# A hybrid DeltaNet and attention step: one triangular inversion split by columns between two engines, masks and an inverse root on VectorE, value products with two heads in turn

## The chip, the core and the metric

The kernel is one program on one core of a Trainium2 chip. The metric is the device time of one execution in microseconds; lower is better. The core's engines each run their own queue of instructions in order and wait for one another through semaphores: TensorE (PE, matmuls and transposes; its weight loads are PEld in the profile), VectorE (DVE), ScalarE (ACT), GpSimd (POOL) and SyncE (SP), on whose queue most of the DMA transfers are issued. Some DMAs are issued from POOL's queue.

## The reference, cut to what matters

Two layers run over 640 tokens, 128 prompt tokens and 512 sample tokens (a grid of 8 rows of 64), of width 1024. Layer 0 mixes tokens by a bidirectional gated DeltaNet (8 heads), layer 1 by neighbourhood attention (16 heads). A gated ConvFFN follows each. All is float32.

```python
# layer 0, per head and direction, chunks of tokens
diff = gc[..., :, None] - gc[..., None, :]            # cumulated log decay
decay = where(lower, exp(where(lower, diff, 0)), 0)
a_mat = where(strict, einsum(kb, kc) * decay, 0)
t_mat = triangular_solve(eye + a_mat, eye, lower=True)
u, w = t_mat @ (vc * bc), t_mat @ (kb * exp(gc))
# then a scan over the chunks with state S: v_new = u - w @ S; o = ...; S = ...
o = rmsnorm(o_f + rev(o_b), norm_g) * silu(z)
# layer 1, per head: latent queries read a window of the grid and all 128 context keys
p = softmax(concat([s_loc + bias (masked), s_ctx]))
out = p_loc @ v_window + p_ctx @ v_ctx
```

## The kernel before

**Staging.** PE does the projections, the FFN and all products. A dense float32 product is three passes (L385 to L387): the weights and the activations are each split into a high part, rounded to the PE's fp32r type, and the rest; ACT makes the high part of a weight tile, DVE the rest by a subtraction (L375, `wl<-wst,wh`).

**Layer 0** has tokens in NBLK = 5 blocks of 128. Its work is a list of steps, written by hand. A letter is a kind of step, a digit the head (for I, the pair of heads):

```python
SCHED = (
    "k1 k0 K0 K1 k2 q0 K2 k3 a1 v1 K3 I0 a1 Q0 v0 V0 I1 q1 M0 v2 Q1 S0 V1 M1 V2 M2 S1 a3 z0 z1 q2 k4 F0 "
    "Q2 k5 F1 K4 K5 v3 z2 V3 a2 q3 Q3 S2 q4 v4 M3 I2 Q4 a2 V4 k6 z3 F2 M4 S3 K6 k7 K7 F3 S4 a1 q5 z4 M5 "
    "q7 a1 v5 Q5 v7 V5 I3 a2 v6 q6 F4 Q6 z5 a1 M6 V6 S5 Q7 z6 S6 M7 V7 F5 S7 a1 F7 F6 a1 z7"
)
```

- k, q, v, z are a head's projections with their convolution (tiles `dkT`, `dqT` and so on); a is a tile of the modulation map.
- **K** is `decay` and `keys`. `decay` (L678) builds a 128x1280 tile `dec` of decay differences in both directions: transposes on PE, additions on DVE (L698), a triangular mask on POOL (L702, two `affine_select` of 128x640, which write -1e30 outside the triangle), and the exponential on ACT (L708). `keys` (L764) turns the keys to tokens (`k3tp`, `k3ts` for head 3; `to_tokens` at L735 to L742), multiplies keys by keys (`kk3p`, `kk3s`, `pair` at L755 to L761), and DVE evicts the product with `dec` into M (L786). MT is its transpose (L791). M's and MT's 32x32 diagonal blocks are stored to a DRAM scratch `md` (L795, SP).
- **I** is `invert` (L799), for two heads at a time: 2 heads x 2 directions x 20 blocks = 80 partitions, each with one unit triangular 32x32 matrix. SP loads `lN` from `md` (L806). Then POOL runs 31 steps of two instructions, a product with broadcast operands into `lP` (L813) and an addition into the inverse `lY` (L819). POOL stores `lY` to `yd` (L820), transposes it by a copy (L821) and stores that to `wd` (L822).
- **M** is `merge` (L824): SP loads the inverted blocks from `yd` and `wd` into M and into small tiles `W6` and `Wx` (L834 to L841; the profile names `W6` as `W`), POOL clears parts of `W6` (L829, L830), and PE combines the 32x32 blocks to 128x128 (L848; tiles `p1` to `p5`, `p` in the profile).
- **Q** multiplies queries by keys into `dec` (L890), **V** scales the values (L900), **S** is the scan over the blocks (L908, tiles `sp`, `sb`), which also stores the final states (L940, SP).
- **F** is `finish` (L976): sums of squares of the output (ACT), then on DVE four small steps and a reciprocal on 128x5 tiles `so`, the power -1/2 on POOL (L989), and the scaling of the output `osb` by it on DVE (L991); PE transposes the result (`ot`, `otp`).

Each engine's order is set by a scheduler, which places an instruction by its priority: steps of kind S, M, K and I are raised by `PR`, and what is raised goes ahead of what is ready with it. Within an engine the order is fixed once built.

**Layer 1** takes the heads in 8 pairs and for each pair four column groups (`attend`, L1243). For a group, PE makes scores against window keys and context keys, for both heads in turn (L1263 to L1273; `skn`, `kc`); DVE and ACT do the softmax (L1184, `sts`); PE transposes the weights (L1312 for the window, `t`; L1315 for the context, `tc`), which are evicted to `ptw` (DVE) and `ptc` (ACT); PE multiplies them by the values into `no` (L1321 to L1330): first all three products of head 0 (two of the window with `vw`, one of the context with `cv`), then the three of head 1. The heads use different halves of the PE array's columns (`tile_position`). The scores of the next group are issued ahead of this group's transposes.

Of the kernel before, what the change touches and what calls it, by code (L numbers as in the profile page):

```python
# [13 lines left out]
F32R = mybir.dt.float32r  # L14
AF = mybir.ActivationFunctionType
# [19 lines left out]
PR = {"S": 2000, "I": 100, "M": 500, "K": 200}  # L35
# [544 lines left out]
class Gdn:  # L580
# [17 lines left out]
    def tokens(self):  # L598
# [4 lines left out]
        for t, sgn in ((self.UT, 1), (self.LT, -1)):  # L603
# [3 lines left out]
            )  # L607
        abT = self.gp.tile([128, W], F32, tag="kT", name="abT", bufs=4)
# [69 lines left out]
    def decay(self, h):  # L678
# [23 lines left out]
        for d, sgn in ((0, 1), (1, -1)):  # L702
            nc.gpsimd.affine_select(
                out=t[:, d], in_=t[:, d], pattern=[[0, NBLK], [sgn, 128]], compare_op=ALU.is_ge, fill=-1e30,
                base=0, channel_multiplier=-sgn,
            )
# [92 lines left out]
    def invert(self, nh, md, yd, wd, name):  # L799
# [5 lines left out]
        P = self.gp.tile([128, 256], F32, tag="lP", name=f"lP{name}", bufs=1)  # L805
# [4 lines left out]
        for i in range(31, 0, -1):  # L810
            n = 32 - i
            pr = P[:L, : i * n].rearrange("p (j c) -> p j c", c=n)
            nc.gpsimd.tensor_tensor(  # L813
                pr,
                N[:L, :i, i : i + 1].to_broadcast([L, i, n]),
                Y[:L, i : i + 1, i:].to_broadcast([L, i, n]),
                ALU.mult,
            )
            nc.gpsimd.tensor_tensor(Y[:L, :i, i:], Y[:L, :i, i:], pr, ALU.add)  # L819
# [156 lines left out]
    def finish(self, h):  # L976
# [4 lines left out]
        so = gp.tile([128, 4, NBLK], F32, tag="so", name=f"so{h}", bufs=2)  # L981
        for b in range(NBLK):
            nc.scalar.activation(sq[:, b], osb[:, b], AF.Square, accum_out=so[:, 0, b : b + 1])
        nc.vector.tensor_scalar(so[:, 1], ssq, 128.0, None, ALU.mult)
        nc.vector.reciprocal(so[:, 2], so[:, 1])
        nc.vector.tensor_tensor(so[:, 0], so[:, 0], so[:, 2], ALU.mult)
        nc.vector.tensor_scalar(so[:, 0], so[:, 0], 1.0 / 128, EPS, ALU.mult, ALU.add)
        nc.vector.tensor_tensor(so[:, 0], so[:, 0], so[:, 1], ALU.mult)
        nc.gpsimd.tensor_tensor(so[:, 3], so[:, 0], self.net.mhalf[:, :NBLK], ALU.pow)  # L989
# [33 lines left out]
    def run(self):  # L1023
# [4 lines left out]
        def step(op, h):  # L1028
# [14 lines left out]
            elif op == "I":  # L1043
                self.invert(2, *scr[h], h)
# [17 lines left out]
        for t in SCHED.split():  # L1062
            if t[0] in PR:
                with net.tc.high_priority(PR[t[0]]):
                    step(t[0], int(t[1]))
# [85 lines left out]
class Na:  # L1151
# [91 lines left out]
    def attend(self, p):  # L1243
# [51 lines left out]
        for cb in range(4):  # L1295
# [25 lines left out]
            for e in range(2):  # L1321
# [322 lines left out]
```

## Time and profile before

| what | value |
|---|---|
| median of 3 runs | 1900.02 us (1899.34 to 1905.55) |
| the profiled execution | 1899.56 us, span 1897.9 us |
| mean granted TensorE clock | 0.977 |
| weight loads on PE (PEld) | 1710.2 us (90%) |
| whole DeltaNet layer's inversions on POOL | 114.5 to 157.0, 188.1 to 227.6, 318.8 to 357.9, 431.9 to 471.9 us |
| DMA, mean | 102 GB/s |

The span is cut by the page into 40 slices of 47 us. Layer 0's mixer fills about the first 12 of them, layer 1's attention lies from 1110 to 1385 us, and most of the rest is FFN, where PE's three passes (L385 to L387) are the costliest groups. In rows of a timeline the columns are the start, the duration, the engine, the line, the operation, the output from the inputs with their sizes, how often, and in brackets the idle time of the engine before it with what ended it. In the list of waits the numbers behind the colon are the sum of the idle time, how often, and the longest.

### The profile page before, as it was taken

The numbers are of one execution on the slowest core, as the hardware profiler recorded it, in microseconds if no ns is written. First come the engines' busy times: TensorE is split into PE (matmuls) and PEld (weight loads), VectorE is DVE, ScalarE is ACT, GpSimd is POOL, SyncE is SP. The second block draws the span as 40 slices with busy tenths as digits, with TensorE's granted clock in tenths as the row PEclk, the third lists the DMA queues.
The fourth block names the chain that finished last, engine by engine and source line by source line (L and its number), as shares of the span: only waits on it lengthen the run. The fifth ranks groups of instructions, "written<-read, shape, count | busy, mean of one in ns | idle before, by whom it ended". The sixth has DMA issues, their size and how long they took to land.

```text
span 1897.9 us, 34312 instructions
## 1 busy us (share of the span) xinstructions
PE 1794.2 (95%) x13587; PEld 1710.2 (90%) x13587; DVE 1207.2 (64%) x2876; ACT 725.2 (38%) x1458; POOL 345.5 (18%) x549
## 2 busy tenths in 40 slices
PE   6886699899999999999999999999999999999998
PEld 5885689799889999999999988888899999999998
DVE  6664467475567999755356699555678743553564
ACT  4444235254353331232234444444453421431443
POOL 1364703518002112100000211111131000000000
PEclk9897899899999999999999999999999999999999
DMA  7223133322242455442223254222233312222231
GB/s 294 73 83 84 36 114 107 92 79 81 63 150 69 161 173 159 140 156 62 87 86 104 76 163 154 78 70 69 69 123 119 121 53 77 87 71 76 88 91 56
DMA packets 102481, 194.16 MB, mean 102 GB/s; under 512 B 39496, under 2 KB 59034, under 8 KB 99560
## 3 DMA queue, kind: packets, MB, share of 16 engines
q1 hardware_dynamic: 93760, 162.88, 27.0%
q0 software_dynamic: 8016, 28.56, 4.7%
q8 instruction: 107, 1.75, 0.4%
q10 hardware_dynamic: 544, 0.52, 0.1%
q14 instruction: 54, 0.44, 0.1%
HBM read 183.09 MB, written 12.46 MB: 103 GB/s over the span
## 4 chain that ended last, share of the span: by engine, by line
PE 48%; DVE 5%; issue 2%; DMA 2%; ACT 1%; POOL 0%; DVEq 0%; POOLq 0%; ACTq 0%
PE duv L385 4%; PE duv L386 4%; PE duv L387 4%; PE dug L385 4%; PE dug L386 4%; PE dug L387 4%; PE rdn L385 4%; PE rdn L386 4%; PE rdn L387 4%; PE dvn L385 1%; DMA bias<-cols 1%; PE dvn L387 1%; PE dvn L386 1%; PE no L1324 1%; PE dqn L385 1%
## 5 line engine op out<-in xcount | busy, mean ns | idle before, releaser
L385 PE MATMUL duv<-hh,whuv 128*128 128x256 f32 (+1 forms) x704 | 217.6, 309 | 6.0 <-DVE yv L442 6.0
L385 PE MATMUL rdn<-F,whdn 128*128 128x384 f32 (+1 forms) x704 | 216.2, 307 | 2.5 <-DVE X L451 2.5
L387 PE MATMUL duv<-hh,wluv 128*128 128x256 f32 (+1 forms) x704 | 217.0, 308 | 0.4 <-DVE wluv L375 0.4
L386 PE MATMUL duv<-hl,whuv 128*128 128x256 f32 (+1 forms) x704 | 217.1, 308 | 0.0
L385 PE MATMUL dug<-hh,whug 128*128 128x256 f32 (+1 forms) x704 | 215.7, 306 | 1.0 <-DVE yg L442 1.0
L386 PE MATMUL dug<-hl,whug 128*128 128x256 f32 (+1 forms) x704 | 215.7, 306 | 0.0
L387 PE MATMUL dug<-hh,wlug 128*128 128x256 f32 (+1 forms) x704 | 215.7, 306 | 0.0
L386 PE MATMUL rdn<-F,whdn 128*128 128x384 f32 (+1 forms) x704 | 215.6, 306 | 0.0
L387 PE MATMUL rdn<-F,wldn 128*128 128x384 f32 (+1 forms) x704 | 215.5, 306 | 0.0
L385 PEld LDWEIGHTS duv<-hh,whuv 128*128 128x128 f32 x704 | 133.4, 189 | 6.6 <-ACT whug L373 3.8
L385 PEld LDWEIGHTS rdn<-F,whdn 128*128 128x128 f32 x704 | 132.4, 188 | 3.1 <-PE rdn L387 1.9
L387 PEld LDWEIGHTS duv<-hh,wluv 128*128 128x128 f32 x704 | 133.2, 189 | 0.8 <-DVE wluv L375 0.8
L385 PEld LDWEIGHTS dug<-hh,whug 128*128 128x128 f32 x704 | 132.5, 188 | 1.2 <-issue 1.2
L386 PEld LDWEIGHTS duv<-hl,whuv 128*128 128x128 f32 x704 | 133.2, 189 | 0.0
L386 PEld LDWEIGHTS rdn<-F,whdn 128*128 128x128 f32 x704 | 132.2, 188 | 0.0
L387 PEld LDWEIGHTS dug<-hh,wlug 128*128 128x128 f32 x704 | 132.2, 188 | 0.0
L387 PEld LDWEIGHTS rdn<-F,wldn 128*128 128x128 f32 x704 | 132.1, 188 | 0.0
L386 PEld LDWEIGHTS dug<-hl,whug 128*128 128x128 f32 x704 | 132.1, 188 | 0.0
L451 DVE SCALAR_TENSOR_TENSOR X<-rdn,mods,X 128x128 f32<-128x128 f32 (+1 forms) x144 | 54.9, 432 | 116.7 <-PE rdn L387 116.5
L373 ACT CAST whdn<-wstdn 128x896 fp32r<-128x896 f32 (+1 forms) x48 | 47.0, 979 | 211.5 <-PE rdn L386 120.9
L373 ACT CAST whug<-wstug 128x1024 fp32r<-128x1024 f32 x44 | 46.2, 1050 | 143.8 <-PE dug L386 120.4
L375 DVE TENSOR_TENSOR wldn<-wstdn,whdn 128x896 fp32r<-128x896 f32 (+1 forms) x48 | 54.3, 1132 | 58.9 <-ACT whdn L373 58.9
(704 smaller groups left out, 4823.7 us busy)
## 6 DMA issues: line engine op xcount, KB each, us to landing
wstuv<-w_up SPq DMA_DIRECT2D x44, 512.0 KB, 3.5
wstug<-w_up SPq DMA_DIRECT2D x44, 512.0 KB, 3.5
adat<-w_ada SPq DMA_DIRECT2D x20, 1024.0 KB, 6.7
adr<-w_adar POOLq DMA_DIRECT2D x80, 256.0 KB, 3.1
wstdn<-w_dn SPq DMA_DIRECT2D x32, 448.0 KB, 3.3
wstdn<-w_dn SPq DMA_DIRECT2D x16, 512.0 KB, 3.5
adr<-w_adar SPq DMA_DIRECT2D x32, 256.0 KB, 2.8
wstqT<-w_gin SPq DMA_DIRECT2D x8, 512.0 KB, 4.4
```

Of the source, the lines that this page charges most:

```text
L373: nc.scalar.copy(wh[:, c], st[:, c])
L375: ins = eng.tensor_tensor(wl[:, c], st[:, c], wh[:, c].bitcast(F32), ALU.subtract).ins
L385: nc.tensor.matmul(out, a, mh, start=first, stop=False)
L386: nc.tensor.matmul(out, a, ml, start=False, stop=False)
L387: ins = nc.tensor.matmul(out, b, mh, start=False, stop=last).ins
L451: nc.vector.scalar_tensor_tensor(x, ps[:, base + c0 : base + c1], self.mod(l, gi, m, v), x, ALU.mult, ALU.add)
L1324: nc.tensor.matmul(out, vw[:n, cb, j, H[e]], pt[:n, 2 * e + j], start=(j == 0), stop=False, tile_position=(0, 64 * e))
```

## The change

There are four edits, and the scheduler's new order that comes from them.

1. **The mask.** One constant tile `far` (0 inside the triangle, -1e30 outside) is built once by POOL. `decay` adds it to `dec` on DVE (two 128x640 additions for a head) in place of the two `affine_select`.
2. **The inversion.** `invert` gets a column `cut`: DVE computes the columns from `cut` on, POOL those before it. The columns of the inverse don't depend on one another, so the two engines need nothing from each other until the store. `CUT` is 24 for inversion 0 and 32 for the others, which stay whole on POOL. Inversion 0 gets a priority of its own, 1000, and the others keep 100. Each engine has its own part of the product tile `lP`.
3. **The inverse root.** `finish` folds the old reciprocal away (the sum of squares is divided by 128, and 128 EPS times the query's sum of squares is added) and takes the inverse root on DVE: a first value from the bits, shifted and subtracted from a constant, and three Newton steps. Five DVE instructions of 128x5 elements and POOL's power become fourteen on DVE.
4. **The value products.** The loop over the three products is now the outer one, that over the two heads the inner one.

```diff
@@ -32,7 +33,8 @@
 HBLK = ((0, 1, 2), (3, 4))
 HN = 384
 NFT = 22
-PR = {"S": 2000, "I": 100, "M": 500, "K": 200}
+CUT = (24, 32, 32, 32)
+PR = {"S": 2000, "I": 100, "I0": 1000, "M": 500, "K": 200}
 WSTB = 2
 EARLY = 4
 UNITS = 6
@@ -604,6 +606,13 @@
             nc.gpsimd.affine_select(
                 out=t, in_=net.ones, pattern=[[sgn, 128]], compare_op=ALU.is_ge, fill=0.0, base=0,
                 channel_multiplier=-sgn,
+            )
+        self.far = self.gs.tile([128, 2, 128], F32, tag="far", name="far")
+        nc.gpsimd.memset(self.far, 0.0)
+        for d, sgn in ((0, 1), (1, -1)):
+            nc.gpsimd.affine_select(
+                out=self.far[:, d], in_=self.far[:, d], pattern=[[sgn, 128]], compare_op=ALU.is_ge, fill=-1e30,
+                base=0, channel_multiplier=-sgn,
             )
         abT = self.gp.tile([128, W], F32, tag="kT", name="abT", bufs=4)
         tmp = [self.gp.tile([128, W], F32, tag="qT", name=f"tk{i}", bufs=2) for i in range(2)]
@@ -699,10 +708,9 @@
                 out, ps[:, : k * 128].rearrange("p (b i) -> p b i", i=128),
                 col.unsqueeze(2).to_broadcast([128, k, 128]), ALU.add,
             )
-        for d, sgn in ((0, 1), (1, -1)):
-            nc.gpsimd.affine_select(
-                out=t[:, d], in_=t[:, d], pattern=[[0, NBLK], [sgn, 128]], compare_op=ALU.is_ge, fill=-1e30,
-                base=0, channel_multiplier=-sgn,
+        for d in range(2):
+            nc.vector.tensor_tensor(
+                t[:, d], t[:, d], self.far[:, d].unsqueeze(1).to_broadcast([128, NBLK, 128]), ALU.add
             )
         f = t.rearrange("p d b i -> p (d b i)")
         nc.scalar.activation(f, f, AF.Exp)
@@ -796,27 +804,31 @@
                     md[q, d].rearrange("b r c -> r b c"), M[s, 0, :, s] if d == 0 else MT[s, :, s]
                 )
 
-    def invert(self, nh, md, yd, wd, name):
+    def invert(self, nh, md, yd, wd, name, cut=32):
+
 
         nc = self.nc
         L = nh * 40
         N = self.gp.tile([128, 32, 32], F32, tag="lN", name=f"lN{name}", bufs=1)
         Y = self.gp.tile([128, 32, 32], F32, tag="lY", name=f"lY{name}", bufs=1)
-        P = self.gp.tile([128, 256], F32, tag="lP", name=f"lP{name}", bufs=1)
+        P = self.gp.tile([128, 336], F32, tag="lP", name=f"lP{name}", bufs=1)
+        P = P[:, 144:], P
         nc.sync.dma_start(N[:L], md.rearrange("h q d b r c -> (h q d b) r c")[:L])
         Yf = Y.rearrange("p r c -> p (r c)")
         nc.gpsimd.memset(Yf[:L], 0.0)
         nc.gpsimd.memset(Yf[:L, 0:1024:33], 1.0)
         for i in range(31, 0, -1):
-            n = 32 - i
-            pr = P[:L, : i * n].rearrange("p (j c) -> p j c", c=n)
-            nc.gpsimd.tensor_tensor(
-                pr,
-                N[:L, :i, i : i + 1].to_broadcast([L, i, n]),
-                Y[:L, i : i + 1, i:].to_broadcast([L, i, n]),
-                ALU.mult,
-            )
-            nc.gpsimd.tensor_tensor(Y[:L, :i, i:], Y[:L, :i, i:], pr, ALU.add)
+            for eng, p, lo, hi in ((nc.vector, P[0], max(i, cut), 32), (nc.gpsimd, P[1], i, cut)):
+                n = hi - lo
+                if n > 0:
+                    pr = p[:L, : i * n].rearrange("p (j c) -> p j c", c=n)
+                    eng.tensor_tensor(
+                        pr,
+                        N[:L, :i, i : i + 1].to_broadcast([L, i, n]),
+                        Y[:L, i : i + 1, lo:hi].to_broadcast([L, i, n]),
+                        ALU.mult,
+                    )
+                    eng.tensor_tensor(Y[:L, :i, lo:hi], Y[:L, :i, lo:hi], pr, ALU.add)
         nc.gpsimd.dma_start(yd.rearrange("h q d b r c -> (h q d b) r c")[:L], Y[:L])
         nc.gpsimd.tensor_copy(N[:L].rearrange("p r c -> p c r"), Y[:L])
         nc.gpsimd.dma_start(wd.rearrange("h q d b r c -> (h q d b) r c")[:L], N[:L])
@@ -979,14 +991,20 @@
 
         sq = self.tmp(f"osq{h}")
         so = gp.tile([128, 4, NBLK], F32, tag="so", name=f"so{h}", bufs=2)
+        V = nc.vector
         for b in range(NBLK):
             nc.scalar.activation(sq[:, b], osb[:, b], AF.Square, accum_out=so[:, 0, b : b + 1])
-        nc.vector.tensor_scalar(so[:, 1], ssq, 128.0, None, ALU.mult)
-        nc.vector.reciprocal(so[:, 2], so[:, 1])
-        nc.vector.tensor_tensor(so[:, 0], so[:, 0], so[:, 2], ALU.mult)
-        nc.vector.tensor_scalar(so[:, 0], so[:, 0], 1.0 / 128, EPS, ALU.mult, ALU.add)
-        nc.vector.tensor_tensor(so[:, 0], so[:, 0], so[:, 1], ALU.mult)
-        nc.gpsimd.tensor_tensor(so[:, 3], so[:, 0], self.net.mhalf[:, :NBLK], ALU.pow)
+        V.tensor_scalar(so[:, 1], ssq, 128 * EPS, None, ALU.mult)
+        V.scalar_tensor_tensor(so[:, 0], so[:, 0], 1.0 / 128, so[:, 1], ALU.mult, ALU.add)
+
+        x, t, y = so[:, 0], so[:, 2], so[:, 3]
+        V.tensor_scalar(t.bitcast(I32), x.bitcast(I32), 1, None, ALU.logical_shift_right)
+        V.tensor_scalar(y.bitcast(I32), t.bitcast(I32), -1.0, float(0x5F3759DF), ALU.mult, ALU.add)
+        V.tensor_scalar(x, x, -0.5, None, ALU.mult)
+        for _ in range(3):
+            V.tensor_tensor(t, y, y, ALU.mult)
+            V.tensor_tensor(t, t, x, ALU.mult)
+            V.scalar_tensor_tensor(y, t, 1.5, y, ALU.add, ALU.mult)
         for b in range(NBLK):
             nc.vector.tensor_scalar(osb[:, b], osb[:, b], so[:, 3, b : b + 1], None, ALU.mult)
         ts, tp = self.g(f"ot{h}"), self.g(f"otp{h}")
@@ -1041,7 +1059,7 @@
                 self.decay(h)
                 self.keys(h, scr[h // 2][0][h % 2])
             elif op == "I":
-                self.invert(2, *scr[h], h)
+                self.invert(2, *scr[h], h, CUT[h])
                 net.lo_engine = nc.vector
             elif op == "Q":
                 self.queries(h)
@@ -1061,7 +1079,7 @@
 
         for t in SCHED.split():
             if t[0] in PR:
-                with net.tc.high_priority(PR[t[0]]):
+                with net.tc.high_priority(PR.get(t, PR[t[0]])):
                     step(t[0], int(t[1]))
             else:
                 step(t[0], int(t[1]))
@@ -1318,16 +1336,16 @@
             nc.vector.tensor_copy(pt[:n], t[:n].rearrange("p (j d) -> p j d", d=128))
             nc.scalar.copy(pc, tc_[:, :256].rearrange("p (j d) -> p j d", d=128))
             yield
-            for e in range(2):
-                out = O[H[e], cb * 128 : cb * 128 + 128]
-                for j in range(2):
+            for j in range(3):
+                for e in range(2):
+                    if j < 2:
+                        v_, p_ = vw[:n, cb, j, H[e]], pt[:n, 2 * e + j]
+                    else:
+                        v_, p_ = self.cv[:, p * 128 + 64 * e : p * 128 + 64 * e + 64], pc[:, e]
                     nc.tensor.matmul(
-                        out, vw[:n, cb, j, H[e]], pt[:n, 2 * e + j], start=(j == 0), stop=False, tile_position=(0, 64 * e)
+                        O[H[e], cb * 128 : cb * 128 + 128], v_, p_, start=(j == 0), stop=(j == 2),
+                        tile_position=(0, 64 * e),
                     )
-                nc.tensor.matmul(
-                    out, self.cv[:, p * 128 + 64 * e : p * 128 + 64 * e + 64], pc[:, e], start=False, stop=True,
-                    tile_position=(0, 64 * e),
-                )
             ps = nxt
         dst = lambda i: A[:, i, SC : SC + 512].rearrange("p (r b c) -> p b c r", b=4, c=16)
         src = O.rearrange("p (b c r) -> p b c r", r=8, c=16)
```

The names' numbers differ between the two kernels, and so do lines; L795 of before is L803 now, L806 is L816, L834 to L841 are L846 to L853, L698 is L707.

The order of SP's queue around the load of inversion 1 (`lN<-md` with the scratch of heads 2 and 3, here 1013). Before, from the loads of head 1's merge into Wx on:

```order
L840 DMA Wx_2002<-wd_720 32x5x32
L841 DMA Wx_2002<-yd_719 32x5x32
L795 DMA md_1013<-M_1303 32x5x32 x4
L836 DMA W_2001<-wd_720 32x5x32
L837 DMA W_2001<-wd_720 32x5x32
L838 DMA W_2001<-yd_719 32x5x32
L839 DMA W_2001<-yd_719 32x5x32
L795 DMA md_1013<-MT_1314 32x5x32 x4
L172 DMA adat_2364<-w_ada 128x2048
L940 DMA out_state<-ns_1861 128x128
L940 DMA out_state<-ns_1871 128x128
L806 DMA lN_1515<-md_1013 80x1024
```

Head 3's stores to `md` (from M_1303 and MT_1314) stood behind the loads of head 0 and nearly all of those of head 1, and the load of inversion 1 behind two stores of the scan's states. Of the change, the stores come at an earlier place, ahead of the loads of both heads:

```order
L803 DMA md_1013<-M_1295 32x5x32 x4
L174 DMA adat_2402<-w_ada 128x2048
L803 DMA md_1013<-MT_1306 32x5x32 x4
L361 DMA wstkT_2634<-w_gin 128x1024
L846 DMA M_784<-yd_727 32x5x32 x4
L850 DMA W_1690<-yd_727 32x5x32
```

and the load right behind the loads of head 1's M and Wx:

```order
L847 DMA M_860<-wd_728 32x5x32
L852 DMA Wx_2040<-wd_728 32x5x32
L853 DMA Wx_2040<-yd_727 32x5x32
L816 DMA lN_1553<-md_1013 80x1024
L848 DMA W_2039<-wd_728 32x5x32
```

So the stores moved from behind these loads to ahead of them, and the load of inversion 1 moved from behind the states' stores to ahead of head 1's four W loads.

The order of DVE's queue where head 3's decay tile (`dec_1244` before, `dec_1240` now) is made. Before:

```order
L791 STREAM_TRANSPOSE MT_1086<-M_1075 128x640
L698 TENSOR_TENSOR dec_1244<-gb_1245,ngc 128x512
L198 TENSOR_TENSOR mods_77<-adp_1164,sm 128x2x2
L442 SCALAR_TENSOR_TENSOR qT_1642<-dqT_1592,sm,qT_1642 128x127
L442 SCALAR_TENSOR_TENSOR qT_1642<-dqT_1592,sm,qT_1642 128x254
L698 TENSOR_TENSOR dec_1244<-gb_1251,ngc 128x512
L698 TENSOR_TENSOR dec_1244<-gb_1257,ngc 128x2x128
```

Now, from the second of the three additions on:

```order
L707 TENSOR_TENSOR dec_1240<-gb_1247,ngc 128x512
L831 TENSOR_TENSOR lY_1317<-lY_1317,lP_1318 80x17x8
L200 TENSOR_TENSOR mods_77<-adp_1160,sm 128x2x2
L825 TENSOR_TENSOR lP_1318<-lN_1316,lY_1317 80x128
L707 TENSOR_TENSOR dec_1240<-gb_1253,ngc 128x2x128
L831 TENSOR_TENSOR lY_1317<-lY_1317,lP_1318 80x16x8
L712 TENSOR_TENSOR dec_1240<-dec_1240,far 128x640
L825 TENSOR_TENSOR lP_1318<-lN_1316,lY_1317 80x120
L712 TENSOR_TENSOR dec_1240<-dec_1240,far 128x640
```

Between any two instructions of head 3's decay stands now an instruction of inversion 0 (`lP` and `lY`), and the two masks (L712) are DVE's own.

More of the change, by code (lines that the diff above doesn't have):

```diff
@@ L14 @@
 F32R = mybir.dt.float32r
+I32 = mybir.dt.int32
 AF = mybir.ActivationFunctionType
```

## The prediction

> **What bounds the kernel now.** I began with the page, to see which engine is full and where it is not.
>
> ```profile
> span 1897.9 us, 34312 instructions
> PE 1794.2 (95%) x13587; PEld 1710.2 (90%) x13587; DVE 1207.2 (64%) x2876; ACT 725.2 (38%) x1458; POOL 345.5 (18%) x549
> ...
> PE   6886699899999999999999999999999999999998
> ...
> POOL 1364703518002112100000211111131000000000
> ```
>
> TensorE is busy for 95% of the span, and from the thirteenth slice (47 us each) on it is full. The change can give something where a slice of the PE row falls short of 9, or where it makes PE's own work shorter. The low slices up to the eleventh are the DeltaNet stage, where POOL is busy. The view of PE's waits names them:
>
> ```profile
> PE kk3s L761 <- ACT k3ts L751: 16.7, 1, 16.7
> PE sb L925 <- ACT osb L957: 14.7, 1, 14.7
> ...
> PE p L848 <- DMA W<-wd: 9.4, 3, 5.1
> ...
> PE q6ts L740 <- ACT qT L732: 4.5, 1, 4.5
> ...
> PE tc L1315 <- DVE sts L1195: 2.1, 5, 0.4
> ```
>
> Three waits blame ACT: 16.7, 14.7 and 4.5 us. Two steps back along the timelines stands POOL both times that I followed it:
>
> ```profile
> 144.38 0.57 POOL L813 TENSOR_TENSOR lP<-lN,lY 80x220 f32<-80x220 f32 x1
> 144.91 1.45 POOL L703 TENSOR_SCALAR_AFFINE_SELECT dec<-dec 128x640 f32<-128x640 f32 x2
> 146.39 1.27 ACT L708 ACTIVATE dec<-dec 128x1280 f32<-128x1280 f32 x1 [16.92 <-POOL dec L703]
> 220.55 1.17 POOL L989 TENSOR_TENSOR so<-so,mhalf 128x5 f32<-128x5 f32 x1
> 221.75 0.54 DVE L991 TENSOR_SCALAR osb<-osb,so 128x128 f32<-128x128 f32 x1 [15.31 <-POOL so L989]
> ```
>
> The mask of head 3 (1.45 us of work) stands in POOL's queue in the middle of inversion 0, and the power of head 0 (1.17 us) in the middle of inversion 1. ACT stood 16.9 us for the first, DVE 15.3 us for the second, and PE behind them. Head 4's power behind inversion 3 makes the 4.5. So moving masks and powers off POOL attacks 36 us of waits by name.
>
> That sum is not the forecast. A wait that goes shows the next latest thing, and here it is the inversions themselves:
>
> ```profile
> 114.53 0.25 POOL L813 TENSOR_TENSOR lP<-lN,lY 80x31 f32<-80x31 f32 x1 [4.68 <-DMA lN<-md]
> 156.75 0.25 POOL L819 TENSOR_TENSOR lY<-lY,lP 80x31 f32<-80x31 f32 x1
> 168.48 0.22 PE L848 MATMUL p<-W,M 32*32 32x32 f32 x2 [3.38 <-DMA W<-wd]
> 174.54 1.82 SPq L795 DMA_DIRECT2D md<-M  x4
> 182.93 0.34 SPq L806 DMA_DIRECT2D lN<-md  x1
> 188.09 0.25 POOL L813 TENSOR_TENSOR lP<-lN,lY 80x31 f32<-80x31 f32 x1 [10.53 <-DMA lN<-md]
> 227.36 0.25 POOL L819 TENSOR_TENSOR lY<-lY,lP 80x31 f32<-80x31 f32 x1
> 237.97 0.24 PE L848 MATMUL p<-W,M 32*32 32x32 f32 x2 [0.89 <-DMA W<-wd]
> ```
>
> Inversion 0 runs from 114.5 to 157.0, its results come back through SP's loads, and PE's merge of head 0 begins 11.5 us after its end. Inversion 1 starts only 31 us after inversion 0 ended, runs 39.5 us to 227.6, and the merge of head 2 begins 10.4 us later, at 238.0. PE waits for data at both merges already. So up to 238 us there is a chain of inversions and loads, and removing 31 us of PE waits beside it gives only what that chain shrinks.
>
> **The change, part by part.**
>
> *Inversion 0.* POOL keeps columns 0 to 23: 46 instructions in place of 62, with 2,300 multiply-adds per row in place of 5,456. DVE gets 62 instructions with 3,156 elements in each of the two passes, 6,312 in all. What they cost on DVE:
>
> ```profile
> L988 DVE TENSOR_TENSOR so<-so 128x5 f32<-128x5 f32 x8 | 1.3, 167 | 0.3
> L897 DVE TENSOR_TENSOR dec<-kq0p,dec 128x128 f32<-128x128 f32 x2 | 0.5, 285 | 0.1
> L779 DVE TENSOR_TENSOR D<-rk,beta 128x5 f32<-128x5 f32 x16 | 2.3, 184 | 0.1
> 154.20 1.11 DVE L786 SCALAR_TENSOR_TENSOR M<-kk3s,D,dec 128x128 f32<-128x128 f32 x4
> 116.45:162.07 45.62, 28.69 (x209) 26.43 (x208) 20.21 (x61) 13.17 (x33) 40.76 (x64) 0.81 0.20 61
> ```
>
> From 5 to 128 elements is 118 ns, about 1 ns an element over a fixed 160. Half of that fixed time lies under the next instruction if that one is independent: four L786 of 0.34 take 1.11, so 0.26 apart. An interleaved instruction occupies about 80 ns plus its elements. The first eight stand alone in the queue and wait for one another (0.195 each plus 0.58 for their elements, 2.1 us); the other 54 cost 4.3 + 5.7 us. Together 12.1. Between them the order now has the work of heads 2 and 3 that DVE did from 116.45 to 162.07, the last row, of which it was busy for 20.2 us, and two new masks of 640 elements (0.7 each). DVE reaches the split's first instruction at about 116.5, so its last ends at 116.5 + 12.1 + 20.2 + 1.4 = 150.2 if nothing disturbs. POOL's half, by 0.26 us plus 1.85 ns an element from its rows (0.25 at 31, 0.57 at 220, plus the 0.08 between two), is 21 us, done before that.
>
> The unknown is what the two engines do to each other. The L779 row has both inputs in SBUF, runs largely beside POOL's inversions, and its mean is 184 against 167 for the same size in L988. That is a small penalty; a few in it were much longer. I take 0.05 us for each of the 62, nearer to that row than to the other end, 3 us: **inversion 0 ends at 153, 4 us earlier.** The bounds: no penalty gives 150 (7 earlier); at the other end each DVE instruction sits out a whole POOL instruction, about 0.5 us, which gives 150 + 31 = 181.
>
> A rule speaks against this part. The Trainium skill, "SBUF — State Buffer", section "Who interferes with whom", says that a VectorE instruction with two SBUF inputs and a GpSimd one that reads SBUF exclude each other for the whole instruction. By it the halves would take turns rather than run together. The 184 ns row agrees only in part, since full turns would show far more than 17 ns.
>
> *SP's queue.* In the order before, the stores of head 3 for inversion 1 (174.5) and its load (182.9) come behind the loads of heads 0 and 1. Now the stores stand ahead of them and the load right behind: where 174.5 was, instead of 182.9. **Inversion 1 starts 8.4 us earlier**, beyond what inversion 0 gives. *Powers* leave POOL: inversion 1 loses 1.2 us, and a buffer clearing moved behind it gives 0.6: **1.8**. Against that, PE's order now puts about 1.1 us less work ahead of the merge of head 2 (half a scan moved behind it, more projection ahead). **Sum up to the merge of head 2: 4.0 + 8.4 + 1.8 − 1.1 = 13.1 us.** PE can follow: it waited 37 us up to there. It will still wait: some 8 to 10 us at kk3s, since its mask now stands behind 48 instructions of the split on DVE, and about 14 at the merge of head 2.
>
> *Later heads.*
>
> ```profile
> 368.41 0.28 PE L848 MATMUL p<-W,M 32*32 32x32 f32 x2 [5.10 <-DMA W<-wd]
> 370.15 0.31 PE L848 MATMUL p<-Wx,M 32*32 32x32 f32 x2 [1.46 <-DMA Wx<-wd]
> 368.75 0.43 SPq L841 DMA_DIRECT2D Wx<-yd  x1
> 370.73 0.26 PE L848 MATMUL p<-Wx,M 32*32 32x32 f32 x1 [0.27 <-DMA Wx<-yd]
> 481.79 0.44 SPq L841 DMA_DIRECT2D Wx<-yd  x1
> 487.31 0.21 PE L848 MATMUL p<-W,M 32*32 32x32 f32 x1
> ```
>
> Inversions 2 and 3 stay whole. Their starts follow PE, so the gain carries on. Before head 4's merge PE waits 5.1 + 1.5 already, and 4 us of its work now precedes head 5's keys, which feed inversion 2: I charge **−2**. The 4.5 at q6ts goes, but head 6's last load is issued at 481.8 and needs about 2 us, as head 4's did (368.75 to 370.73), so its merge (487.3) had 3.5 to spare, less 1.6 for keys that move later: **+2.5**. The new inverse root is thirteen small dependent DVE instructions (L988: 167 plus 35 apart, 2.6 us) for four and a power (2 us). In the middle the scans and projections on PE hide it; without that cover it costs 0.6 a head. At the last head nothing covers it: **−0.6**.
>
> *Value products.*
>
> ```profile
> 1113.27 0.71 PE L1324 MATMUL no<-ptw,vw 92*64 92x128 f32 x6
> ...
> 1114.34 0.69 PE L1270 MATMUL s<-skn,sqn 64*128 64x248 f32 x4
> 1114.87 0.39 PE L1270 MATMUL s<-kc,sqn 64*128 64x128 f32 x4
> 1115.18 0.33 PE L1312 MATMUL t<-ident,Ps 128*124 128x128 f32 x1
> ```
>
> Each product is two records, so a group of six products is twelve, and takes 1.07 us to the next work. The scores with the context keys have the heads in turn already: four records of the same 128 columns in 0.31, pairs running side by side. Six pairs at 0.11 each plus the tail of 0.2 make 0.80. So 0.27 a group, 32 groups, 8.6 us. Five groups already end in a wait for DVE (tc, above), and shorter products lengthen such waits. With as many that are near it I take off 2: **6.6.** The bounds are 0 (all absorbed) and 8.6.
>
> **Sum.** 13.1 − 2 + 2.5 − 0.6 + 6.6 = 19.6. The profiled execution took 1899.56 us (span 1897.9), the median of the three runs is 1900.02, within 0.5. 1899.6 − 19.6 = **1880.0**.
>
> **Rivals.**
>
> *A: the halves take turns.* DVE's instructions each wait for about a third of a POOL instruction, 0.16 us in all: inversion 0 ends at 150 + 10 = 160, not 153. Then 19.6 − 7 = 12.6, **1887**. For it: instructions of this kind have not run side by side at this size in this trace. Against it: 184 to 167. Chance 0.20.
>
> *B: the value products give nothing*, since DVE's softmax ends last in most groups: 13.0, **1886.6**. Against it: in that stage PE is 98% busy.
>
> ```profile
> 115.00:152.00 37.00, 20.23 (x151) 19.01 (x149) 13.77 (x37) 12.46 (x27) 33.24 (x54) 0.82 0.22 68
> 240.00:363.00 123.00, 121.92 (x1145) 108.61 (x1143) 78.65 (x226) 56.53 (x158) 46.75 (x79) 1.00 0.32 102
> 1110.00:1385.00 275.00, 270.85 (x2047) 240.11 (x2047) 184.26 (x541) 120.88 (x299) 43.83 (x85) 1.00 0.31 96
> ```
>
> Chance 0.08.
>
> *C: better.* No penalty between the halves (3 more), no loss at head 4 (2), and products in full (2): 26.6, **1873**. The rows above add a reason: the granted clock was 0.82 in the stretch with the long wait and 1.00 in the full one, so fewer waits also mean faster matmuls. Chance 0.13.
>
> *D: slower.* DVE's queue becomes the chain. Each of the 62 DVE instructions waits for a whole POOL instruction (0.5 us), and the head 3 mask, the weight subtractions and kk3's evictions queue behind them. Inversion 0 ends at 181; both merges and inversion 1 move with it: 28 us against 19.6, **1908**. It decides from 0.05 + 19.6/62 = 0.37 us of waiting each. The 184 ns mean speaks against it. Chance 0.04.
>
> **How the numbers follow.** My forecast (1874 to 1886) has the remaining 0.55. A measurement of this kernel tells about 0.3%, 5.7 us, from no change: above 1894 is not faster. Of A 0.02 ends there, of B none, of D all; of the forecast's own tail I give 0.04. Faster 0.90, same 0.06, slower 0.04. The range reaches to A, B and C: 1869 to 1892.
>
> **What would show it.** In the new trace: no AFFINE_SELECT on dec and no power on so; DVE's lP and lY instructions near 0.16 us plus 1 ns an element (right) or up to 0.5 longer (A, D); the last lY of inversion 0 near 153; the load of inversion 1 within 18 us of that; a wait of 8 to 10 at kk3s, and some 14 at head 2's merge in place of the 14.7 at sb; value groups of 0.8 us instead of 1.07. I am wrong if the merge of head 2 does not start 10 to 17 us earlier, or if the stage of attention keeps its 275 us.

## The result, and the profile after

| | before | changed |
|---|---|---|
| median | 1900.02 us | 1880.83 us (1879.30 to 1889.29, 5 runs) |
| ratio to before | | 0.9905, interval 0.9886 to 0.9923 |
| span of the profiled execution | 1897.9 us | 1879.1 us |

Two executions further down that took far longer than the others of their kernels (3052.5 us of the changed kernel, 5233.0 us of a variant) are in no median here.

Where the 18.8 us of span went is read from the view of busy time by stretch. The columns are the stretch, its length, then busy time and number of instructions of PE, PEld, DVE, ACT and POOL, the granted clock, and DMA. The first stretch goes from the first transpose of `decay` (`gb`) to the last of `finish` (`ot`) and holds DeltaNet after its inputs, the second from the first value product to the last. Of the kernel before:

```profile
76.40:549.10 472.70, 420.06 (x3890) 381.14 (x3889) 278.43 (x811) 203.58 (x591) 192.68 (x315) 0.94 0.28 83
1113.30:1380.00 266.70, 262.55 (x1995) 232.24 (x1994) 177.92 (x525) 115.05 (x284) 42.25 (x83) 1.00 0.30 93
```

Of the changed kernel:

```profile
76.00:536.90 460.90, 421.11 (x3890) 380.50 (x3889) 314.38 (x960) 201.98 (x591) 158.19 (x275) 0.95 0.29 86
1098.00:1358.70 260.70, 254.15 (x1995) 223.30 (x1994) 178.35 (x525) 115.22 (x284) 41.92 (x83) 1.00 0.31 95
```

The two gains are of different kinds. DeltaNet got 11.8 us shorter with PE just as busy (420 and 421 us): what went is idle time of PE, 52.6 to 39.8 us. Attention got 6.0 shorter although PE's idle time grew from 4.2 to 6.6 us: there PE's own work shrank, by 8.4. Outside the two stretches 1.0 us is left over.

PE's waits now, in the list of the changed kernel:

```profile
PE p L860 <- DMA W<-wd: 24.6, 2, 14.4
...
PE tc L1333 <- DVE sts L1213: 3.8, 6, 0.7
PE kk3p L769 <- ACT k3tp L759: 3.1, 1, 3.1
...
PE q6ts L748 <- ACT qT L740: 0.9, 1, 0.9
...
PE sb L937 <- ACT osb L969: 0.8, 1, 0.8
```

The waits by name that POOL caused (16.7, 14.7 and 4.5) are down to 4.8. The wait at the merges' loads went from 9.4 to 24.6. In order of time, the steps that the prediction named:

```profile
152.10 0.15 DVE L831 TENSOR_TENSOR lY<-lY,lP 80x8 f32<-80x8 f32 x1
169.72 0.37 SPq L816 DMA_DIRECT2D lN<-md  x1
173.20 0.25 POOL L825 TENSOR_TENSOR lP<-lN,lY 80x31 f32<-80x31 f32 x1 [1.42 <-DMA lN<-md]
211.07 0.25 POOL L831 TENSOR_TENSOR lY<-lY,lP 80x31 f32<-80x31 f32 x1
222.52 0.31 PE L860 MATMUL p<-W,M 32*32 32x32 f32 x2 [14.39 <-DMA W<-wd]
257.03 0.33 PE L1012 MATMUL otp<-ident,osb 128*128 128x128 f32 x1
362.19 0.28 PE L860 MATMUL p<-W,M 32*32 32x32 f32 x2 [10.18 <-DMA W<-wd]
473.31 0.55 PE L748 MATMUL q6ts<-ident,qT 128*128 128x128 f32 x3 [0.89 <-ACT qT L740]
```

Inversion 0 ends at 152.3, inversion 1 runs from 173.2 to 211.3 (before 188.1 to 227.6), and head 2's merge starts at 222.5 instead of 238.0.

### The profile page after: what moved, and what is told of

Same layout as the page of the kernel before. It is cut to its first block, busy times and chain, and to the rows that moved or that the text cites. A ratio compares the mean times of both kernels' runs of the same rounds, so it can differ in the third digit from the quotient of the medians.

```text
span 1879.1 us, 34407 instructions
## 1 busy us (share of the span) xinstructions
PE 1784.7 (95%) x13587; PEld 1698.5 (90%) x13587; DVE 1244.9 (66%) x3026; ACT 723.9 (39%) x1458; POOL 311.1 (17%) x512
## 4 chain that ended last, share of the span: by engine, by line
PE 48%; DVE 5%; issue 3%; DMA 2%; ACT 1%; POOL 0%; DVEq 0%; POOLq 0%; ACTq 0%
PE duv L387 4%; PE duv L388 4%; PE duv L389 4%; PE dug L387 4%; PE dug L388 4%; PE dug L389 4%; PE rdn L387 4%; PE rdn L389 4%; PE rdn L388 4%; PE dvn L387 1%; PE dvn L389 1%; PE dvn L388 1%; PE no L1345 1%; PE dqn L387 1%; PE s L1288 1%
```

## The experiments

Three groups of runs, each beside the kernel before on its own chip (medians of before 1898.1, 1897.4 and 1896.4 us). The kernel before ran there from 1889 to 1910 us, so the ratios' intervals are 0.3 to 0.6% wide. The stage from the first `gb` to the last `ot`, read from each run's profile, tells more: it contains the same work in all runs, PE is busy in it for 419 to 424 us in each, and the same code came out at 472.7 and 469.2 (before, and with other value products alone) and at 460.9 and 458.1 (the change, twice). So differences of up to 3.5 us in it are scatter. The stage less PE's busy time is PE's idle time; it was 52.6 us before and 39.8 in the changed kernel.

| run | ratio to before | stage, us | of it PE busy | PE idle |
|---|---|---|---|---|
| value products alone | 0.9973 (0.9955 to 0.9991) | 469.2 | 418.9 | 50.3 |
| the change without the split | 0.9990 (0.9973 to 1.0006) | 474.6 | 420.5 | 54.1 |
| the same, stores of head 3 early | 0.9987 (0.9971 to 1.0002) | 477.0 | 421.0 | 56.0 |
| split alone | 0.9979 (0.9963 to 0.9996) | 469.9 | 419.5 | 50.4 |
| the change again | 0.9930 (0.9903 to 0.9958) | 458.1 | 420.8 | 37.3 |
| the change, masks on POOL | 0.9938 (0.9918 to 0.9958) | 465.2 | 418.8 | 46.4 |
| the change, power on POOL | 0.9934 (0.9909 to 0.9959) | 464.9 | 424.1 | 40.8 |
| load of inversion 1 first | 0.9919 (0.9891 to 0.9948) | 456.9 | 420.4 | 36.5 |
| and odd heads' loads on POOL | 0.9875 (0.9855 to 0.9895) | 454.3 | 420.4 | 33.9 |
| and inversion 2 split | 0.9908 (0.9888 to 0.9928) | 455.7 | 421.9 | 33.8 |

### Value products alone

The kernel before with the change's fourth edit.

```diff
-            for e in range(2):
-                for j in range(2): ...
+            for j in range(3):
+                for e in range(2): ...
```

> The kernel before with the value products' loops exchanged, nothing else. Theory (the prediction's 0.27 us a group, with waits for DVE given back): PE's own time on the tile no falls by 8.6 us, some 2.4 of it come back as longer waits for the softmax, so 6.2 us faster, 1893.8. Rival B: DVE sets the groups and nothing is gained, 1900. Third possibility: the full 8.6, 1891.4.

Median 1893.11. The gain of 5 us agrees with 6.2; its interval (1.7 to 8.5 us) leaves out 0, and 8.6 only just. In its profile it is 260.4 us from the start of the first value product to that of the last, as in the changed kernel (before 266.5); rival B falls.

### Without the split

```diff
-CUT = (24, 32, 32, 32)
+CUT = (32, 32, 32, 32)
```

> The changed kernel with inversion 0 whole on POOL again (CUT 32 in all places); masks, inverse root and value products as changed. SP's queue then has head 3's stores and the load of inversion 1 where they stood before. Theory (the chain of inversions and loads sets the merge of head 2; the split carries both the shorter inversion and the earlier place of the stores): the named waits at kk3s and sb are gone, and a wait of 10 us or more stands at head 2's merge, which starts within 4 us of the 238.0 of before; in all 1888 to 1891. Rival (the masks and powers on POOL were what cost): merge at 223, in all about 1881 to 1883, so that the split is worth nothing.

Median 1894.80. Its list of PE's waits:

```profile
PE p L860 <- DMA W<-wd: 42.2, 3, 21.5
```

and its merges of heads 0 and 2 in the timeline:

```profile
168.45 0.28 PE L860 MATMUL p<-W,M 32*32 32x32 f32 x2 [21.51 <-DMA W<-wd]
241.17 0.31 PE L860 MATMUL p<-W,M 32*32 32x32 f32 x2 [14.47 <-DMA W<-wd]
```

Of the waits at kk3s, sb and q6ts 2.8 us are left at sb and 0.9 at q6ts; the other 32 stand again at the merges. The stage is 474.6, not shorter than before (472.7, 469.2): masks and inverse root on DVE give nothing by themselves, which is even less than I had expected of them (1888 to 1891). The rival, in which the split is worth nothing, falls.

### Without the split, but with the early stores

```diff
+                with self.net.tc.high_priority(3000 if h == 3 else 0):
                     nc.sync.dma_start(md[q, d]..., M... if d == 0 else MT...)
```

> As nosplit, but the stores of head 3 and the load of inversion 1 are given the early place in SP's queue by a priority, as in the changed kernel. Theory: of the 15 us at head 2's merge some 8 to 10 are the place of stores and load, the rest the shorter inversion; so merge of head 2 at about 228 to 230, in all 1882 to 1886. Rival (the shorter inversion is all): as nosplit, 1888 to 1891.

The edit raises only the stores; the load of inversion 1 follows them, from 184.5 to 176.6. Inversion 1 starts 9.7 us earlier than without the priority (181.3 and 191.0), and head 2's merge 10.5 earlier (230.6 and 241.2). The time does not move (1895.80, stage 477.0). The time is that of the run before, as the rival had it, but not for the rival's reason, since the merge did come earlier. It starts earlier because less of PE's work stands ahead of it (115.6 us of busy time since the first `gb`, 123.4 without the priority). PE's idle time up to head 4's merge stays the same (49.1 and 48.7), and the work that had stood ahead comes behind. The start of a merge is no measure of progress where the order moves work past it.

### The split alone

The kernel before with the change's `invert`, its `CUT` and the priority of inversion 0.

```diff
-PR = {"S": 2000, "I": 100, "M": 500, "K": 200}
+CUT = (24, 32, 32, 32)
+PR = {"S": 2000, "I": 100, "I0": 1000, "M": 500, "K": 200}
```

> The kernel before with inversion 0 split at column 24 and its priority, nothing else: masks and powers stay on POOL, value products as before. Theory: inversion 0 ends by 155, SP's queue has the early place, so the merge of head 2 starts 9 to 13 us earlier and the whole takes 1889 to 1893. Rival (a split is of no use while POOL's queue still holds the masks and powers, since its half waits with them): within 4 us of 1900.

Median 1893.90, 4 us less by the ratio, with an interval of 0.8 to 7 us that doesn't decide between theory and rival. Its waits:

```profile
PE sb L930 <- ACT osb L962: 17.1, 1, 17.1
...
PE kk3p L762 <- ACT k3tp L752: 7.2, 1, 7.2
```

Inversion 1 starts at 180.0 (before 188.1), but the power of head 0 now waits for its end, and PE waits 17.1 us at sb. Inversion 0 ends at 159.2, not by 155, and head 2's merge starts at 232.5, 5.5 us earlier and not 9 to 13. The stage is 469.9, inside the scatter of the two profiles of the kernel before (472.7, 469.2).

### The whole change again, and without one of its parts

The changed kernel; the changed kernel with the two `affine_select` of before in `decay`; and the changed kernel with the old inverse root of `finish`.

> The changed kernel as it is, beside the runs below on their chip. If the parts simply added, the value products (5 to 6 us), the split (4) and masks with inverse root (0 or below) would make 9 to 11 us, ratio 0.9945. Theory (masks with inverse root and split are worth something only together, since PE's own way to the merge of head 2 and the inversions' chain run side by side and the later of the two sets the merge): 17 to 19 us, ratio 0.990 to 0.991, as it was measured first.

```diff
-            nc.vector.tensor_tensor(t[:, d], t[:, d], self.far[:, d]..., ALU.add)
+            nc.gpsimd.affine_select(out=t[:, d], in_=t[:, d], ..., fill=-1e30, ...)
```

> The changed kernel with the masks of head decays on POOL again (affine_select as before); split, inverse root and value products as changed. Theory: the mask holds kk3 for some 7 us as in the run with the split alone, but PE makes that up in the wait of 14 us at head 2's merge; the sb wait is gone, so head 2's merge starts at 222 to 228 and 1 to 4 us are lost against the whole change. Rival (the mask is the partner that the split needs): merge of head 2 at 232 or later, sb wait or kk3 wait of 15 us, 8 us or more lost.

```diff
-        V.tensor_scalar(t.bitcast(I32), x.bitcast(I32), 1, None, ALU.logical_shift_right)
-        ...
+        nc.vector.reciprocal(so[:, 2], so[:, 1])
+        ...
+        nc.gpsimd.tensor_tensor(so[:, 3], so[:, 0], self.net.mhalf[:, :NBLK], ALU.pow)
```

> The changed kernel with the old inverse root again (power on POOL, reciprocal on DVE); split, masks and value products as changed. Theory: the power of head 0 stands inside inversion 1, PE waits some 15 us at sb and 4.5 at q6ts, head 2's merge starts at 231 or later without a wait for DMA of more than 5 us, and 7 to 10 us are lost against the whole change. Rival (the inverse root is not needed): head 2's merge at 222 to 226, less than 3 us lost.

Medians 1881.50, 1885.25 and 1885.94; the times do not tell the three apart. The profiles say more. With the masks on POOL, inversion 0 ends at 157.2 and PE waits 7.0 at kk3p; head 2's merge starts at 226.5, as the theory had it, and PE is idle for 46.4 us of the stage, 7 to 9 more than in the two profiles of the changed kernel. With the power on POOL, PE's list has

```profile
PE sb L937 <- ACT osb L969: 17.6, 1, 17.6
```

and the merge starts at 227.5, without the wait at it, as I expected, but earlier than the 231 that I named. Each costs 4 to 7 us of the stage's 458 to 461, a little more than the scatter. For the masks all of it is idle time of PE. For the power only 1 to 3.5 us are (40.8 against 39.8 and 37.3), since the wait at sb takes the place of the one at the merge; the rest is PE's busy time, 3 us longer. So the masks are needed beside the split; for the inverse root these profiles show it less clearly.

Without the split the two bring the stage from about 471 to 474.6 and PE's idle time from about 51 to 54.1. With it they bring the stage from 469.9 to 459.5 and the idle time from 50.4 to 38.6: worth nothing or 10 us, by whether the split is there. By the times the three parts alone would make 5.1 + 4.0 − 3.2 = 5.9 us (the last from 0.9990 and 0.9973). Together they made 13 (0.9930) and 18 (0.9905). Each of these figures has an interval of 3 to 5 us to either side, so it is the profiles that carry this.

### What each half of inversion 0 costs alone

One execution of each; DVE's columns are left out in the first, POOL's in the second.

```diff
-                if n > 0:
+                if n > 0 and (cut == 32 or eng is nc.gpsimd):
```

> The changed kernel with DVE's columns 24 to 31 of inversion 0 left out of the computation; POOL's columns stay. It shows POOL's half alone. Theory (the two engines disturb each other only now and then): the sum of POOL's 46 instructions falls from 22.0 to about 20, and those of one size agree within 0.05 us. Rival A (they take turns): it falls by 8 us or more, to 14 or below.

> The changed kernel with POOL's columns 0 to 23 of inversion 0 left out of the computation; DVE's stay. It shows DVE's half alone. Theory: DVE's 62 instructions take 147 ns plus 1.03 ns an element each, in sum 15.5 us against 17.9 in the changed kernel, so that the neighbour costs 0.04 us each, and inversion 0 ends at most 3 us earlier. Rival A (turns): 9 us or less in sum, or an end 7 us earlier.

DVE's products (L825) of inversion 0 in the view of busy time, restricted to that line, where DVE's column stands ahead of POOL's. The changed kernel, then in a second fence the kernel with DVE's half alone:

```profile
112.00:160.00 48.00, 8.85 (x31) 9.97 (x23) 0.89 0.40 118
```

```profile
112.00:160.00 48.00, 7.83 (x31) 0.00 (x0) 0.93 0.40 119
```

With the additions (9.02 and 7.88) DVE's 62 take 17.9 us beside POOL and 15.7 alone: 35 ns each. The 43 that ran while POOL's half was running have all of it, 50 ns each, unevenly: 15 took 0.07 to 0.22 us longer, the other 28 at most 0.06. POOL's 46 take 22.0 beside DVE's half and 21.5 without it, but both sums hold instructions that other work on DVE made longer (up to 2.06 us). Without the seven places where one of the two was over 0.8 us, it is 15.8 and 15.0. Rival A at the size that these runs named for it (8 us and more) falls.

POOL's half alone shows something else. It ends inversion 0 after 26.1 us instead of 37.4. But from the start of inversion 0 to that of inversion 1 it is 55.2 us instead of 58.3, and the stage is 464.5, not shorter than with the whole change. Its timeline:

```profile
144.57 0.23 POOL L831 TENSOR_TENSOR lY<-lY,lP 80x23 f32<-80x23 f32 x1
```

```profile
160.74 2.90 SPq L803 DMA_DIRECT2D md<-M  x4
...
169.03 0.37 SPq L816 DMA_DIRECT2D lN<-md  x1
```

Inversion 1's load goes out 24 us after the end of inversion 0 (17.5 in the changed kernel), because this kernel's order has head 3's stores among the merge loads again, as it was before. Of eleven microseconds off the inversion the place of these transfers in a queue took back eight. The rest of this kernel's order differs too, so the length of the stage can't be laid to them alone.

### Going on from there

In the changed kernel SP issues 24 merge loads of two heads ahead of inversion 1's load. First this load is given the inversion's priority:

```diff
-PR = {"S": 2000, "I": 100, "I0": 1000, "M": 500, "K": 200}
+PR = {"S": 2000, "I": 100, "I0": 1000, "I1": 1000, "M": 500, "K": 200}
```

> The changed kernel with priority 1000 for inversion 1 too: its load of lN goes in SP's queue ahead of nearly all the loads of the merges of heads 0 and 1 (it is issued at some 161 us, not 170). Theory (the chain of loads and inversions sets head 2's merge, where PE waits 14 us): inversion 1 starts 8 to 9 us earlier, at about 165, head 2's merge at about 214, and 5 to 9 us are gained on the changed kernel, ratio to before 0.986 to 0.988. Rival (merges of heads 0 and 1 come later and PE has nothing else to do, or the gain is lost at head 4): within 2 us of the changed kernel.

It is issued at 163.6, and from the start of inversion 0 to that of inversion 1 it is 48 us instead of 58. Median 1878.99, stage 456.9; the gain on the changed kernel is 2 us by the ratios, within what the two tell apart, as the rival had it. Head 2's merge starts at 221.6, not 214. The reason stands in SP's queue after inversion 1:

```profile
206.07 0.25 POOL L831 TENSOR_TENSOR lY<-lY,lP 80x31 f32<-80x31 f32 x1
```

```profile
217.27 0.43 SPq L847 DMA_DIRECT2D M<-wd  x1
217.74 0.43 SPq L846 DMA_DIRECT2D M<-yd  x1
...
219.78 0.32 SPq L848 DMA_DIRECT2D W<-wd  x1
```

Head 3's M loads stand ahead of head 2's W, 0.43 us each, and the merge starts 15.3 us after the inversion's end (11.2 in the changed kernel). So the odd heads' loads go to POOL's queue, which is idle then:

```diff
+        q_ = nc.gpsimd if h in (3, 5, 7) else nc.sync
-            nc.sync.dma_start(M[s, 0, :, s], v(yd, q, 0))
+            q_.dma_start(M[s, 0, :, s], v(yd, q, 0))
         ...
```

> The kernel i1first with the merge loads of heads 3, 5 and 7 issued on POOL's queue, not SP's, so that head 3's loads no longer stand between head 2's in SP's queue. Theory (SP's queue after inversion 1, 0.43 us a load, sets head 2's merge now): the merge starts 10 us after inversion 1's end, not 15, and 2 to 5 us are gained on i1first. Rival (PE's own work or head 4's merge sets the end): the merge comes earlier, and the whole stays within 1 us of i1first.

Median 1874.28 and ratio 0.9875, the lowest of all; its interval leaves out both ratios of the changed kernel and that of the kernel with only the load first, though it overlaps two of their three intervals. The merge starts 11.3 us after inversion 1's end (204.0 to 215.3). The stage is 454.3, 2.6 shorter than with only the load first, which is inside the scatter (the profiled execution was the slowest of the five, 1879.50), so where the rest of the gain lies is not shown. PE's work in the stage is 420.4, so 34 us of waits are left.

> As i1_oddpool, with inversion 2 split at column 24 as well. Theory (head 4's merge waits 10 us for inversion 2): inversion 2 gets 2 to 6 us shorter and so does that wait; 2 to 5 us are gained on i1_oddpool. Rival (DVE's queue is late there, its split instructions wait behind other work, since inversion 2 has a low priority): inversion 2 is not shorter and nothing is gained.

```diff
-CUT = (24, 32, 32, 32)
+CUT = (24, 32, 24, 32)
```

The rival is right. POOL's half of inversion 2 ends first, DVE's long after it:

```profile
325.15 0.23 POOL L831 TENSOR_TENSOR lY<-lY,lP 80x23 f32<-80x23 f32 x1
347.49 0.16 DVE L831 TENSOR_TENSOR lY<-lY,lP 80x8 f32<-80x8 f32 x1
```

Inversion 2 takes 45.7 us instead of 39.4, since DVE's instructions of low priority stand between other work. Median 1880.13.

## Why the prediction was right, step by step

**The sum.** Forecast 1880.0, measured 1880.83. Forecast for DeltaNet 13.0, measured 12.2 at the last transpose of `finish`; forecast for the value products 6.6, measured 6.0. The two large steps hold, the chain of inversions and loads and the paired products. That the sum came within 1 us is in part luck. Behind head 2's merge the forecast runs 4 to 5 us ahead of what was measured, and most of that comes back behind head 4's merge. In this table, in us, the second pair is the run with value products alone against the change again, counted from the first `gb`:

| gain up to | forecast | measured | second pair |
|---|---|---|---|
| head 2's merge | 14.2 (before the −1.1) | 15.4 | 14.3 |
| head 0's first output transpose | 13.1 | 9.3 | 8.7 |
| head 4's merge | 11.1 | 6.2 | 4.7 |
| head 6's merge | 13.6 | 11.1 | 9.6 |
| last output transpose | 13.0 | 12.2 | 11.1 |

On the second chip the change also gained only 13 us (0.9930), and the interval there leaves out the forecast's 19.6.

**The waits by name are not the gain.** This carried the forecast, and the runs show it: without the split, 32 of the 36 us of waits blamed on POOL go and none of the stage.

**Inversion 0** was put at 153 and ended at 152.3; the penalty, put at 0.05 us for each instruction, is 0.035 on DVE's side. **Inversion 1** was to start 12.4 us earlier and started 14.9 earlier. **The wait at kk3** was put at 8 to 10 us, with the mask behind 48 instructions of the split. That was a miscount: in DVE's order 32 stand ahead of the first mask of head 3 and 33 ahead of the second, and the wait was 3.1. The wait at head 2's merge was put at 14 and measured 14.4.

**What comes behind head 2's merge is the step that was mis-sized.** I charged −1.1 for moved work. The merge came 15.4 us earlier, but head 0's first output transpose, the next common point, only 9.3 (266.3 to 257.0). The stretch between the two, before, after, and in the changed kernel with the power on POOL:

```profile
237.90:266.30 28.40, 27.91 (x317) 22.55 (x318) 14.31 (x39) 9.26 (x24) 1.63 (x3) 1.00 0.43 134
```

```profile
222.50:257.00 34.50, 33.47 (x344) 28.31 (x344) 19.99 (x63) 9.76 (x28) 0.45 (x2) 0.89 0.39 111
```

```profile
227.50:258.00 30.50, 30.50 (x344) 25.53 (x344) 18.41 (x53) 9.99 (x29) 1.62 (x3) 1.00 0.38 119
```

After the change it holds 27 more matmuls and 5.6 us more of PE's busy time: 36 of the scan (`sb`, `o`) moved behind the merge, against 16 of the projection `dkT` ahead of it. The third row separates two causes. It has the same matmuls but for two or three, at a granted clock of 1.00, and no wait at the merge. So the moved work is 2.6 us (30.5 against 27.9), and the other 3.0 come with the clock of 0.89, behind a wait of 14.4 us that PE did not have there before. In all fourteen profiles the clock of this stretch is 1.00 where PE waited under 1 us at the merge (four of them) and 0.77 to 0.94 where it waited 11 to 19 us (ten). In the kernel before, the slow clock lay ahead of the merge, behind the wait of 14.7 us at sb (0.59 over the next 4 us). It moved with the wait. So up to this point 6.2 us were lost in place of 1.1: the prediction priced the moved work too low and the clock behind the new wait not at all. A merge that starts earlier overstates the gain by both.

**Later heads.** Head 4 was put at −2 and took 3.1 off the gain (9.3 to 6.2). Head 6 was put at +2.5 and gave 4.9 by its merge: 3.6 of the wait at q6ts, and 1.3 because the clock behind that wait was 0.59 before and is 1.00 now. Of PE's work from q6ts to the merge, before and then after:

```profile
483.10:487.30 4.20, 4.20 (x21) 4.09 (x21) 0.57 (x3) 1.99 (x11) 0.00 (x0) 0.59 0.30 48
```

```profile
473.30:476.20 2.90, 2.89 (x22) 2.52 (x22) 0.66 (x3) 1.96 (x11) 0.00 (x0) 1.00 0.28 42
```

The last head was put at −0.6. From head 6's merge on 1.1 us were gained, nearly all of it PE's busy time (59.6 to 58.6) and not waits; why is not shown.

**Value products.** 8.6 less work of PE and 2 us of longer waits were forecast; 8.4 less and 2.4 more idle time were measured. The tc wait grew from 2.1 to 3.8.

**The rule on ports.** The Trainium skill, "SBUF — State Buffer", section "Who interferes with whom", lets a VectorE instruction with two SBUF inputs and a GpSimd one that reads SBUF block each other wholly. This case's trace agrees for the masks and leaves it open for the split. In the changed kernel there are instructions of the split beside POOL's that take what they take alone, though their records overlap:

```profile
124.33 0.35 DVE L831 TENSOR_TENSOR lY<-lY,lP 80x184 f32<-80x184 f32 x1
124.56 0.45 POOL L825 TENSOR_TENSOR lP<-lN,lY 80x140 f32<-80x140 f32 x1
```

```profile
124.08 0.34 DVE L831 TENSOR_TENSOR lY<-lY,lP 80x184 f32<-80x184 f32 x1
```

(the second fence is DVE's half alone). But a record also holds time that does not grow with the size (DVE's half alone: 0.15 us at 80x8, 0.34 at 80x184), so overlapping records do not show that the two read at the same moment. Only the size is settled: 50 ns a pair, not a whole turn. Beside the two new masks of head 3 on DVE, a POOL addition of a size that took 0.40 to 0.44 in other places took 2.06, some 1.6 more, about as long as both masks:

```profile
133.53 2.06 POOL L831 TENSOR_TENSOR lY<-lY,lP 80x119 f32<-80x119 f32 x1
133.58 0.81 DVE L712 TENSOR_TENSOR dec<-dec,far 128x640 f32<-128x640 f32 x1
...
134.51 0.81 DVE L712 TENSOR_TENSOR dec<-dec,far 128x640 f32<-128x640 f32 x1
```

So whole turns would have been the wrong price for the split. But moving head 3's mask to DVE did not free POOL of it: POOL lost some 1.6 us where its own two `affine_select` had taken 1.45. The masks of the other seven heads met no work on POOL. What makes the two cases differ (80 or 128 partitions, length, broadcast operands) was not tried.

## What to carry to other kernels

Where two chains run side by side to the same point, shortening one shows as a longer wait on the other: price the parts together, and test them together, since each alone may measure as nothing. Count PE's idle time between two points that have the same work between them, not the start of a stage that the order can move work past, and read the granted clock behind each wait with it. And look at the DMA queue that links two stages: the place of a few transfers there took back eight of eleven microseconds of a shorter inversion.

## What the runs showed of the hardware beyond that

The six products of a group of values, with the heads in turn, issue in pairs, as the scores do: PE's busy time fell by 8.4 us over 32 groups, 0.26 us a group, with the instructions' own durations unchanged (median 273 ns for a window product before and after). Behind a long wait PE runs at a lower granted clock for some microseconds. In eight profiles (before, value products alone, without the split, split alone, the change twice, and each of its two parts taken back) a wait of 13 to 18 us at sb or at head 2's merge is followed by 0.50 to 0.62 over the next 4 us and by 1.00 from 12 us on; behind 4.5 us at q6ts it was 0.59 over 4.2 us. The program's start scattered more than expected: the first transpose of `decay` came at 75.1 to 77.6 us in eleven profiles and at 80.9 in three, with the same 397 matmuls ahead of it (PE busy for 53 to 55 us, and for 58 in the three), as much as some of the effects studied here.
